# A hybrid attention block on one core: product 21 of a paired head moved between u and q, hooks moved by a product, and the first output block reordered

## The chip, the core and the metric

The kernel runs on one core of a Trainium2 chip: TensorE (matrix products into PSUM, an accumulator memory in banks of 512 fp32 values per partition), VectorE, ScalarE and GpSimd (element work), SyncE and GpSimd issue DMAs. The metric is the device time of one execution in microseconds; the kernel before ran three timed times, and once under the hardware profiler.

## The reference, cut to what matters

```python
h = _rmsnorm(x, norm_g[l])                      # x: (1, 512, 2048) float32
proj = h @ w_in[l]                              # q, k, v, z of both groups of heads, gates
...
qa = _rope(_heads(qa, 8, 128))                  # heads 0 to 7: three attentions, mixed by gates
o_a = gates[..., 0:1]*o_cmp + gates[..., 1:2]*o_sel + gates[..., 2:3]*o_win
y_a = o_a.reshape(B, S, WIDTH_A) * jax.nn.silu(za)
qb = _rope(_heads(qb, 16, 64))                  # two of these make one "head" of 128 columns
o_b = _banded_attention(qb, kb, vb, 128, sink)  # window of 128, a sink per head
y_b = o_b.reshape(B, S, WIDTH_B) * jax.nn.silu(zb)
x = x + jnp.concatenate([y_a, y_b], axis=-1) @ w_out[l]
return _rmsnorm(x, final_g)
```

All is fp32. The kernel splits each fp32 operand into a high and a low word and makes each product as three matrix products of words (`mm3`, L126 to L129: high x high, low x high, high x low).

## The kernel before, in words

The 512 tokens lie in SBUF as normalized words `xh`, `xl`. A first part (to 195 us) makes keys, values, compressed keys and gates. Then come 16 heads of 128 columns: 0 to 7 of the first kind, 8 to 15 of the second kind (two small heads side by side).

For heads 1 to 14 the q and the z projection are one 2 x 2 block product with seven multiplications in place of eight (a Strassen-Winograd scheme), in `pair(h)` at L685. The products are named p, 22, 21, 12, w, u, q. Each is 24 matmuls of 128 x 256 (`prod`, L661) on a sum of weight blocks. A weight block (128 x 1024) comes by DMA into a `raw` tile; `unit` splits it (ScalarE copies the high words `whi`, L641; VectorE subtracts for the low words `wlo`, L642); VectorE adds blocks to one another (`plus`, L698/L699). The seven products go into halves of two banks, `pa` and `pb`; ScalarE copies a product out (L731, L737, L747) or VectorE adds it to partial sums (L699). 22 is made first, then p, 21, 12, w, u, q. p, 12 and w lie in `pa`, 22, 21, u and q in `pb`. With u the query projection is whole: VectorE and GpSimd rotate it (L760 to L762), `q_split` makes words `qh`, `ql` (heads 1 to 7: ScalarE L501, GpSimd L502), `qb_split` the words `qs` of heads 8 on (ScalarE L870, VectorE L873, then four DMAs on SyncE's queue, L882, that move the low words to other partitions). `tags` hands out the five `raw` rooms; a room is free again when its last split or sum has read it. Heads up to 9 are narrow here (four rooms, sums made in place), heads 10 on wide (`h > 9`, five rooms, one more sum made by an accumulating DMA).

Behind its pair a head of the first kind runs `attn_a` (scores L565, softmax, transposes L603, value products L609 to L611). A head of the second kind is held: its parts are hung into the next head's pair as hooks, each issued behind a product (scores L903/L904 by `s0`, `s1`; divisions L922/L924; value products L942, L943, L948 by `k0` to `k3`, `end`). Head 15 has plain projections (`plain`, L775) with the same hooks.

Behind the last head comes the output projection. The first 512 columns (`wo0`, L1110) are plain: 8 units of 48 matmuls. Meanwhile `combos` (L1028) makes sums of y's blocks and their words, in place of y. Then `xs` rows are added to the products and squared (L1124 to L1127), and for n = 1 to 3 (L1149) the next 512 columns each are again seven products p, 22, 12, u, ... with weights from `wos`; `summed` (L1181) loads two blocks on top of one another (a load by SyncE, then an accumulating one by GpSimd, L1185), into tiles `ch`.

The written order is not the order of the engines: a scheduler with a simulated timeline orders each engine's instructions by what is ready in its model; `issue_after` binds an instruction behind another. PSUM is guarded bank by bank: a product that begins in a bank waits for what an engine still reads from that bank.

Of the kernel before, what the change touches and what calls it, by code (L numbers as in the profile page):

```python
# [17 lines left out]
P = 128  # L18
# [17 lines left out]
def hybrid_block(ctx, tc, xT, xtm, w0, w1s, w2s, wz, wq, wkb, wo0, wos, cw1, cw2, cpos, rope, tabs, sinks, gT, fg, out):  # L36
# [39 lines left out]
    raws = [0]  # L76
# [448 lines left out]
    pso = poa.enter_context(tc.tile_pool(name="pso", bufs=1, space=PSUM, side="left"))  # L525
    wks = ctx.enter_context(ExitStack())
# [146 lines left out]
    tags = ["raw2", "raw0", "raw1", "raw3"]  # L673
# [11 lines left out]
    def pair(h, early=(), hooks=None):  # L685
# [14 lines left out]

        if wide:
            c1, c2, c5, c3, c4 = tags
            tags[:] = c4, c1, c2, c3, c5
        else:
            c1, c2, c4, c3 = tags
            tags[:] = (c4, c1, c3, c2) if h < 9 else (c4, c1, "raw4", c3, c2)
        pa, pb = [psp.tile([P, S], F32, name="pj", tag="pj") for e in range(2)]
# [7 lines left out]
        if wide:  # L715
            d = wb.tile([P, 256], F32, name="dd", tag="dd")
        x1 = load(c1, 3)
        u0 = unit(x1)
        x2 = load(c2, 0)
        u3 = unit(x2)  # L720
        if wide:
            sm = load(c5, 0, 2)
        else:
# [17 lines left out]
        if wide:  # L741
            x4 = load(c4, 2, 3)
# [9 lines left out]
        plus(d, d, pa[:, H1])  # L752
# [3 lines left out]
        prod(pb[:, H1], u5, "u", True)  # L756
        plus(qv[:, H1], d, pb[:, H1])
# [56 lines left out]
    for h in range(8):  # L814
        if h < FIRST:
# [5 lines left out]
            with tc.issue_after(last["dma"]):  # L821
                first.append(load_quarter(wq[0], tags[0], 3))
                forms_back(0, lows)
                forms_back(1, lows)
            for c, quarter in zip(tags[1:], (0, 2, 1)):
# [28 lines left out]
    vb3 = wb.tile([P, P], F32, name="vb3")  # L854
    nc.sync.dma_start(cosB, ropeb[0])
# [11 lines left out]
    def qb_split(t1, direct=False):  # L867
# [3 lines left out]
        if not direct:  # L871
            lo = wk.tile([P, S], F32R, name="qlo", tag="t2", bufs=1)
            dve.tensor_tensor(out=lo, in0=t1, in1=q2[0].bitcast(F32), op=ALU.subtract)  # L873
        for v, qs in enumerate(q2):
            for half in range(2):
                r = half * 64 + v * 32
                d = half * 64 + 32 - v * 32
                if direct:
                    dve.tensor_tensor(out=qs[d:d + 32], in0=t1[r:r + 32], in1=qs[r:r + 32].bitcast(F32),
                                      op=ALU.subtract)  # L880
                else:
                    nc.sync.dma_start(qs[d:d + 32].bitcast(F32), lo[r:r + 32].bitcast(F32))  # L882
        return q2

    def attention(i, q2):
# [6 lines left out]
        def softmax(part):  # L892
# [26 lines left out]
            for e, v, ns in parts:  # L919
                tv = tts[2 * part + e][:, v, ns]  # L920
                if i < 6:
                    act.activation(tv, tv, AF.Copy, scale=dn[:, e, v:v + 1])  # L922
                else:
                    dve.tensor_scalar(tv, tv, dn[:, e, v:v + 1], None, op0=ALU.mult)  # L924
# [513 lines left out]
```

## Time and profile before

| | us |
|---|---|
| three timed executions | 831.44, 834.11, 838.43 (median 834.11) |
| the profiled execution | 830.96 |
| its span | 829.1 |
| TensorE clock granted, mean | 0.996 |
| matmuls busy (share of span) | 796.3 (96%) |
| weight loads busy | 746.1 (90%) |
| VectorE | 688.4 (83%) |
| ScalarE | 521.9 (63%) |
| GpSimd | 91.3 (11%) |

The profiled execution is one run, and its views are given in us from the start of its span. A matmul's row is longer than its share of TensorE's time, since matmuls are pipelined; what counts is the distance of two starts. Idle time of an engine is told with what ended it: `[0.84 <-PE pj L129]` is 0.84 us of idle time that ended when an instruction of line 129 on TensorE, writing `pj`, was done. PEld are the weight loads of TensorE. The stage of the paired heads is about 222 to 600 us, head 15 and the last held head 600 to 700, the output projection the rest.

### The profile page before, as it was taken

To read this page: it belongs to the slowest core of one execution; us is meant where nothing else is said; L and a number is where in the kernel's file an instruction comes from. 1 tells how busy PE (TensorE), PEld (TensorE's weight loads), DVE (VectorE), ACT (ScalarE), POOL (GpSimd) and SP (SyncE) were. 2 spreads that over 40 slices of the span, in tenths; PEclk is the share of its full clock that TensorE was granted. 3 is DMA by queue.
4 is the path that set the end of the run, shared out by engine and by line. 5 is a ranking of instruction groups with operands and counts; after the bars stand their busy time and mean duration, and the time that the engine had idled before them with its cause. 6 is when DMAs were issued, how large, how long until landed. Compare 5 with 4: busy or idle time off the path is not lost.

```text
span 829.1 us, 15441 instructions
## 1 busy us (share of the span) xinstructions
PE 796.3 (96%) x5782; PEld 746.1 (90%) x5782; DVE 688.4 (83%) x1283; ACT 521.9 (63%) x1088; POOL 91.3 (11%) x75
## 2 busy tenths in 40 slices
PE   8999999999999999999999999999999998899996
PEld 7788898988999999999999899899988887899996
DVE  6869785975798989997997898889987998678894
ACT  6734456662577867866777478676875657443545
POOL 3510002022010011010110012101110000100000
PEclk9999999999999999999999999999999999999999
DMA  8665886899712215323213585666674236697835
GB/s 308 210 204 166 277 283 209 250 307 359 251 44 95 77 42 165 109 61 113 85 58 115 159 205 153 168 174 153 179 261 158 77 102 245 189 262 192 267 66 203
DMA packets 60475, 145.03 MB, mean 175 GB/s; under 512 B 6257, under 2 KB 19825, under 8 KB 60401
## 3 DMA queue, kind: packets, MB, share of 16 engines
q1 hardware_dynamic: 56944, 132.00, 48.2%
q0 software_dynamic: 3168, 11.54, 8.2%
q8 instruction: 45, 0.74, 0.4%
q10 hardware_dynamic: 288, 0.52, 0.2%
q14 instruction: 30, 0.24, 0.1%
HBM read 121.65 MB, written 20.55 MB: 172 GB/s over the span
## 4 chain that ended last, share of the span: by engine, by line
PE 69%; DVE 10%; DMA 10%; ACT 4%; issue 4%; SPq 1%; POOL 1%; ACTq 0%; DVEq 0%; POOLq 0%
PE pj L127 12%; PE pj L129 12%; PE pj L128 12%; PE bank L129 4%; PE bank L128 3%; PE bank L127 3%; PE sp L565 3%; PE oa L128 3%; PE oa L129 3%; PE oa L127 3%; DMA rw<-wos 2%; DMA qs<-qlo 2%; DMA raw<-wq 1%; DVE wlo L642 1%; DMA ch<-wos 1%
## 5 line engine op out<-in xcount | busy, mean ns | idle before, releaser
L127 PE MATMUL pj<-xh,whi 128*128 128x256 f32 (+1 forms) x560 | 170.7, 305 | 2.7 <-ACT whi L641 1.5
L129 PE MATMUL pj<-xh,wlo 128*128 128x256 f32 (+1 forms) x560 | 170.1, 304 | 3.0 <-DVE wlo L642 2.9
L128 PE MATMUL pj<-xl,whi 128*128 128x256 f32 (+1 forms) x560 | 169.0, 302 | 0.0
L641 ACT ACTIVATE whi<-raw 128x1024 fp32r<-128x1024 f32 x98 | 102.8, 1054 | 46.7 <-PE pj L128 19.4
L642 DVE TENSOR_TENSOR wlo<-raw,whi 128x1024 fp32r<-128x1024 f32 x98 | 122.0, 1249 | 8.8 <-ACT whi L641 8.4
L129 PEld LDWEIGHTS pj<-xh,wlo 128*128 128x128 f32 x560 | 105.5, 188 | 8.9 <-DVE wlo L642 4.0
L127 PEld LDWEIGHTS pj<-xh,whi 128*128 128x128 f32 x560 | 105.5, 188 | 8.5 <-ACT whi L641 1.9
L128 PEld LDWEIGHTS pj<-xl,whi 128*128 128x128 f32 x560 | 105.4, 188 | 4.4 <-issue 0.2
L97 DVE TENSOR_TENSOR wlo<-raw,whi 128x512 fp32r<-128x512 f32 (+2 forms) x74 | 80.7, 1095 | 33.8 <-ACT whi L96 33.6
L96 ACT ACTIVATE whi<-raw 128x1024 fp32r<-128x1024 f32 (+1 forms) x73 | 65.3, 900 | 57.9 <-PE pj L128 14.9
L127 PE MATMUL pj<-pu,whi 128*128 128x256 f32 x224 | 63.9, 285 | 0.4 <-DVE zr L699 0.3
L129 PE MATMUL pj<-pu,wlo 128*128 128x256 f32 x224 | 63.4, 283 | 0.0
L128 PE MATMUL pj<-pu,whi 128*128 128x256 f32 x224 | 63.2, 282 | 0.0
L699 DVE TENSOR_TENSOR raw<-raw 128x1024 f32<-128x1024 f32 x46 | 58.0, 1261 | 0.2
L762 POOL TENSOR_TENSOR t<-t,t 128x512 f32<-128x512 f32 x14 | 24.4, 1745 | 248.1 <-DVE sums L584 79.6
L128 PE MATMUL oa<-wlo,xh 128*128 128x256 f32 (+1 forms) x168 | 50.3, 299 | 1.5 <-DVE wlo L1016 0.9
L127 PE MATMUL oa<-whi,xh 128*128 128x256 f32 (+1 forms) x168 | 50.0, 300 | 0.9 <-ACT whi L1015 0.9
L129 PE MATMUL oa<-whi,xl 128*128 128x256 f32 (+1 forms) x168 | 50.0, 299 | 0.0
L127 PEld LDWEIGHTS pj<-pu,whi 128*128 128x128 f32 x224 | 42.2, 189 | 1.4 <-DVE zr L699 1.3
L533 ACT ACTIVATE ph<-tp 128x512 fp32r<-128x512 f32 x56 | 32.1, 590 | 16.9 <-PE tp L936 8.6
L129 PEld LDWEIGHTS pj<-pu,wlo 128*128 128x128 f32 x224 | 42.3, 189 | 0.5 <-DVE wlo L642 0.2
L128 PEld LDWEIGHTS pj<-pu,whi 128*128 128x128 f32 x224 | 42.2, 188 | 0.1
(364 smaller groups left out, 2347.0 us busy)
## 6 DMA issues: line engine op xcount, KB each, us to landing
raw<-wq SPq DMA_DIRECT2D x65, 512.0 KB, 4.3
raw<-cw SPq DMA_DIRECT2D x16, 512.0 KB, 4.9
raw<-wos SPq DMA_DIRECT2D x12, 512.0 KB, 4.9
raw<-wq POOLq DMA_DIRECT2D x10, 512.0 KB, 5.6
rw<-wos SPq DMA_DIRECT2D x10, 512.0 KB, 5.7
xr<-xT SPq DMA_DIRECT2D x16, 256.0 KB, 5.3
raw<-w SPq DMA_DIRECT2D x8, 512.0 KB, 4.4
fd<-ft SPq DMA_DIRECT2D x4, 1024.0 KB, 5.8
```

Source lines behind the costliest of these rows:

```text
L96: last["hi"] = act.activation(hi[:, :width], rw[:, :width], AF.Copy).ins
L97: last["lo"] = dve.tensor_tensor(out=lo[:, :width], in0=rw[:, :width], in1=hi[:, :width].bitcast(F32), op=ALU.subtract).ins
L127: pe.matmul(ps, ah, bh, start=first, stop=False, skip_group_check=go_on)
L128: pe.matmul(ps, ah, bl, start=False, stop=False, skip_group_check=go_on)
L129: recent["mm"] = pe.matmul(ps, al, bh, start=False, stop=last, skip_group_check=go_on).ins
L533: act.activation(ph, tp, AF.Copy)
L565: pe.matmul(sp[:, a:b], qq[:, qs], kk[0][:, ko:ko + b - a], start=pi == 0, stop=pi == 2)
L641: act.activation(hi, src, AF.Copy)
L642: last["lo"] = dve.tensor_tensor(out=lo, in0=src, in1=hi.bitcast(F32), op=ALU.subtract).ins
L699: return dve.tensor_tensor(out=out, in0=a, in1=b, op=op).ins
L762: pool.tensor_tensor(out=qv, in0=qv, in1=t2, op=ALU.add)
```

## The change

In `pair`, the order of products becomes p, 22, 12, w, u, 21, q. u and q move to the half of the bank that p and 12 had, 21 stays with 22, and the two banks change roles from head to head. The hooks move with the order: what hung behind 21 now hangs behind 12, and so on, so that each hangs behind a product of the same number (third, fourth, ...). The order of loads and room tags follows. All divisions of the held heads are ScalarE's. Head 15's q words go through the four DMAs as those of heads 8 to 14 do. Behind the last head the tile `raw3` lies in a room that stays to the end; the first block sum of n = 1 is loaded into it (SyncE and accumulating GpSimd DMA) behind head 15's z; `combos` writes the words of u and q into rooms that are free since the last scores (`cmb`, `cmc`); and the additions of `xs` rows with their squares (`first_rows`) stand behind the splits of the second product's weights of n = 1.

```diff
@@ weights, pools
-        home = {"raw3": lambda: wk, "raw4": lambda: wb}.get(tag, lambda: wp)()
+        home = {"raw3": lambda: chp, "raw4": lambda: wb}.get(tag, lambda: wp)()
...
+    chp = ctx.enter_context(sb("chp"))
+    weights("raw3")
...
-    tags = ["raw2", "raw0", "raw1", "raw3"]
+    tags = ["raw0", "raw2", "raw1", "raw3"]
@@ pair
-        pa, pb = [psp.tile([P, S], F32, name="pj", tag="pj") for e in range(2)]
+        banks = [psp.tile([P, S], F32, name="pj", tag="pj") for e in range(2)]
+        pa, pb = banks if h % 2 else banks[::-1]
...
+        prod(pa[:, H0], u3, "p", True)
+        act.activation(d, pa[:, H0], AF.Copy)
         prod(pb[:, H0], u0, "22", True)
-        act.activation(d, pb[:, H0], AF.Copy, scale=-1.0)
-        x3 = load(c3, 1)
-        prod(pa[:, H0], u3, "p", True)
-        plus(d, d, pa[:, H0])
-        u2 = unit(x3)
-        prod(pb[:, H0], u2, "21", False)
-        act.activation(zr[:, H1], pb[:, H0], AF.Copy)
-        plus(jj, d, zr[:, H1])
-        after("21")
+        plus(d, d, pb[:, H0], ALU.subtract)
         u4 = unit(sm)
...
         plus(sm, sm, x1)
+        x3 = load(c3, 1)
         prod(pa[:, H0], u4, "12", False)
         act.activation(qv[:, H0], pa[:, H0], AF.Copy)
-        plus(jj, jj, qv[:, H0], ALU.subtract)
+        plus(jj, d, qv[:, H0], ALU.subtract)
         after("12")
         u1 = unit(x4)
         prod(pa[:, H1], u1, "w", True)
-        plus(d, d, pa[:, H1])
+        plus(qv[:, H1], d, pa[:, H1])
         after("w")
         u5 = unit(sm)
         plus(sm, sm, x3)
-        prod(pb[:, H1], u5, "u", True)
-        plus(qv[:, H1], d, pb[:, H1])
+        prod(pa[:, H0], u5, "u", True)
+        plus(qv[:, H1], qv[:, H1], pa[:, H0])
...
         qq = q_split(qv) if h < 8 else qb_split(qv)
+        after("u")
+        u2 = unit(x3)
+        prod(pb[:, H0], u2, "21", False)
+        act.activation(zr[:, H1], pb[:, H0], AF.Copy)
+        plus(jj, jj, zr[:, H1])
+        after("21")
         u6 = unit(sm)
-        after("u")
-        prod(pb[:, H1], u6, "q", False)
-        plus(jj, jj, pb[:, H1])
+        prod(pa[:, H0], u6, "q", False)
+        plus(jj, jj, pa[:, H0])
@@ heads 8 on
-                if i < 6:
-                    act.activation(tv, tv, AF.Copy, scale=dn[:, e, v:v + 1])
-                else:
-                    dve.tensor_scalar(tv, tv, dn[:, e, v:v + 1], None, op0=ALU.mult)
+                act.activation(tv, tv, AF.Copy, scale=dn[:, e, v:v + 1])
...
-            hooks = {"21": [j["s0"]], "12": [j["s1"]], "w": [j["k0"]], "u": [j["k2"], j["k3"]], "q": [j["k1"], end]}
+            hooks = {"12": [j["s0"]], "w": [j["s1"]], "u": [j["k0"]], "21": [j["k2"], j["k3"]], "q": [j["k1"], end]}
...
-    a15 = attention(7, qb_split(q_rope(qp, cosB, sinB, dve), True))
+    a15 = attention(7, qb_split(q_rope(qp, cosB, sinB, dve)))
@@ behind the last head
+    ch1 = weights("raw3")
+    with tc.issue_after(last["dma"]):
+        nc.sync.dma_start(ch1, wos[0][0, 0])
+    pool.dma_start(ch1, wos[0][2, 0], accum_op=ALU.add)
...
+    uq = {(nm, m): [(cmb if m < 4 else cmc).tile([P, 2, 256], F32R, name=f"{nm}{e}{m}") for e in "hl"]
+          for m in (2, 0, 6, 4) for nm in "qu"}
...
-        for nm, src in (("p", a11), ("u", a12), ("q", a21)):
+        for nm, src in (("p", a11), ("q", a21), ("u", a12)):
...
-    for t in range(NQ):
-        v = xs0[t // 2][:, t % 2, :]
-        dve.tensor_tensor(out=v, in0=acc[t], in1=v, op=ALU.add)
-        square(ssq[:, t, 1:2], v)
+    def first_rows():
+        for t in range(NQ):
+            v = xs0[t // 2][:, t % 2, :]
+            with tc.issue_after(last["lo"]):
+                dve.tensor_tensor(out=v, in0=acc[t], in1=v, op=ALU.add)
+            square(ssq[:, t, 1:2], v)
...
-            product(bb, [halves(r) for r in r22], "22", True)
+            u22 = [halves(r) for r in r22]
+            if n == 1:
+                first_rows()
+            product(bb, u22, "22", True)
         gg = scratch()
-        ch = summed(chain, 0, 2)
+        ch = summed(chain, 0, 2, [ch1] if n == 1 else ())
```

TensorE, last pair (head 14), kernel before, from the end of u to the start of q. `pj_7186` is `pb`; `pu11` are the words that u multiplies, `VH`, `VL` those of q; `tp` are transposes of the held head.

```order
L127 MATMUL pj_7186<-pu11_1364,whi_7424 128x256
L128 MATMUL pj_7186<-pu11_1364,whi_7424 128x256
L129 MATMUL pj_7186<-pu11_1364,wlo_7425 128x256
L936 MATMUL tp_7411<-ident_61,ttb_7288 128x128
L936 MATMUL tp_7411<-ident_61,ttb_7296 128x128
L936 MATMUL tp_7411<-ident_61,ttb_7288 128x128
L936 MATMUL tp_7411<-ident_61,ttb_7296 128x128
L127 MATMUL pj_7186<-VH_1383,whi_7469 128x256
L128 MATMUL pj_7186<-VL_1384,whi_7469 128x256
```

The change there. `pj_7193` is `pa`, which u has just left and q enters; `pj_7192` is `pb`.

```order
L129 MATMUL pj_7192<-xh_108,wlo_7447 128x256
L127 MATMUL pj_7192<-xh_108,whi_7446 128x256
L128 MATMUL pj_7192<-xl_109,whi_7446 128x256
L129 MATMUL pj_7192<-xh_108,wlo_7447 128x256
L127 MATMUL pj_7192<-xh_108,whi_7446 128x256
L128 MATMUL pj_7192<-xl_109,whi_7446 128x256
L129 MATMUL pj_7192<-xh_108,wlo_7447 128x256
L933 MATMUL tp_7433<-ident_61,ttb_7299 128x128
L933 MATMUL tp_7433<-ident_61,ttb_7307 128x128
L933 MATMUL tp_7433<-ident_61,ttb_7299 128x128
L933 MATMUL tp_7433<-ident_61,ttb_7307 128x128
L127 MATMUL pj_7193<-VH_1383,whi_7496 128x256
```

What moved: seven matmuls of 21 now stand between u and q, beside the four transposes; the other 17 of 21 stand ahead of u.

TensorE, a narrow pair of the change (head 4), from the end of 12 to the start of w. `pj_3545` is `pa` with 12 and then w, `pj_3544` is `pb` with 21; `sp` are scores of the head before.

```order
L129 MATMUL pj_3545<-xh_108,wlo_3614 128x256
L567 MATMUL sp_3442<-KH0_119,qh_3308 128x288
L567 MATMUL sp_3442<-KH0_119,qh_3308 128x512
L567 MATMUL sp_3442<-KL0_121,qh_3308 128x288
L567 MATMUL sp_3442<-KL0_121,qh_3308 128x512
L567 MATMUL sp_3442<-KH0_119,ql_3309 128x288
L567 MATMUL sp_3442<-KH0_119,ql_3309 128x512
L127 MATMUL pj_3544<-xh_108,whi_3715 128x256
L128 MATMUL pj_3544<-xl_109,whi_3715 128x256
L127 MATMUL pj_3545<-xh_108,whi_3647 128x256
```

What moved: before, 21 was whole ahead of 12; now its first two matmuls stand between 12's scores and w, the rest behind w.

VectorE, first output block behind the last head, kernel before. `xs00`, `xs01` are the rows to be added, `pl`, `ul`, `xl` low words of y, `wlo` those of weights (from `raw`: product p; from `rw`: 22; from `ch`: 12).

```order
L1126 TENSOR_TENSOR xs00_7951<-oa_7980,xs00_7951 128x512
L1126 TENSOR_TENSOR xs00_7951<-oa_7981,xs00_7951 128x512
L1016 TENSOR_TENSOR pl_7959<-y3_7549,ph_7958 128x512
L1126 TENSOR_TENSOR xs01_7952<-pj_7982,xs01_7952 128x512
L1126 TENSOR_TENSOR xs01_7952<-pj_7983,xs01_7952 128x512
L1016 TENSOR_TENSOR wlo_8316<-raw_8313,whi_8315 128x1024
L1016 TENSOR_TENSOR ul6_8273<-y3_7549,uh6_8272 128x512
L1016 TENSOR_TENSOR xl_109<-y3_7549,xh_108 128x2x256
L1016 TENSOR_TENSOR wlo_8376<-rw_8369,whi_8375 128x1024
L1016 TENSOR_TENSOR wlo_8380<-rw_8371,whi_8379 128x1024
L1016 TENSOR_TENSOR wlo_8440<-ch_8432,whi_8439 128x1024
```

The change there. `raw_7891` is the sum that is loaded early.

```order
L1018 TENSOR_TENSOR ul6_7983<-y3_7556,uh6_7982 128x512
L1018 TENSOR_TENSOR xl_109<-y3_7556,xh_108 128x2x256
L1018 TENSOR_TENSOR wlo_8379<-rw_8372,whi_8378 128x1024
L1018 TENSOR_TENSOR wlo_8383<-rw_8374,whi_8382 128x1024
L1130 TENSOR_TENSOR xs00_7966<-oa_8011,xs00_7966 128x512
L1130 TENSOR_TENSOR xs00_7966<-oa_8012,xs00_7966 128x512
L1130 TENSOR_TENSOR xs01_7967<-pj_8013,xs01_7967 128x512
L1130 TENSOR_TENSOR xs01_7967<-pj_8014,xs01_7967 128x512
L1018 TENSOR_TENSOR wlo_8452<-raw_7891,whi_8451 128x1024
```

What moved: the four additions stand behind the low words for 22 and ahead of those for 12; the low words for p and most of y's stand further up.

## Rows read from the trace of the kernel before

**Rows 1.** Page, part 1: busy us (share of span) and instructions of each engine.
```profile
PE 796.3 (96%) x5782; PEld 746.1 (90%) x5782; DVE 688.4 (83%) x1283; ACT 521.9 (63%) x1088; POOL 91.3 (11%) x75
```

**Rows 2.** Stretches: from:to and length, busy us (x instructions), TensorE clock, DMA share, GB/s.
```profile
222.00:600.00 378.00, 365.65 (x3029) 356.28 (x3029) 336.77 (x721) 277.25 (x663) 42.41 (x30) 1.00 0.42 121
300.00:330.00 30.00, 29.08 (x242) 28.45 (x242) 28.19 (x60) 21.62 (x55) 3.35 (x3) 1.00 0.35 116
625.00:675.00 50.00, 49.36 (x257) 41.47 (x256) 44.57 (x106) 31.84 (x69) 0.00 (x0) 1.00 0.33 104
700.00:725.00 25.00, 20.20 (x170) 19.41 (x169) 18.72 (x22) 13.21 (x20) 3.05 (x4) 1.00 0.74 230
725.00:750.00 25.00, 25.00 (x223) 25.00 (x222) 17.49 (x18) 12.75 (x19) 2.21 (x3) 1.00 1.01 274
```

**Rows 3.** Waits of TensorE: line <- releaser: us in total, times, longest.
```profile
PE oa L128 <- DVE wlo L1016: 3.9, 3, 2.0
PE pj L129 <- DVE wlo L642: 2.9, 4, 0.9
PE spb L903 <- DMA qs<-qlo: 2.5, 3, 1.2
PE pj L127 <- ACT whi L641: 1.5, 2, 0.9
PE oa L127 <- ACT whi L1015: 0.9, 1, 0.9
PE pj L127 <- DVE t L699: 0.8, 2, 0.6
```

**Rows 4.** Timeline, last pair, u to q: start, us, engine, line, operation, tiles [idle before <-releaser].
```profile
613.83 0.42 DVE L699 TENSOR_TENSOR t<-dd,pj 128x256 f32<-128x256 f32 x1 [0.84 <-PE pj L129]
614.30 0.38 PE L127 MATMUL pj<-VH,whi 128*128 128x256 f32 x1
```

**Rows 5.** Single lines: count, shortest/median/longest ns, first and last start, forms.
```profile
L641 ACT ACTIVATE whi<-raw x98: 1040/1054/1074, 199.3 to 607.7; 128x1024 fp32r<-128x1024 f32 x98
L731 ACT ACTIVATE t<-pj x9: 357/368/386, 214.6 to 461.1; 128x256 f32<-128x256 f32 x9
L565 PE MATMUL sp<-KH,qh x64: 274/295/398, 210.2 to 443.8; 128*128 128x288 f32 x32, 128*128 128x256 f32 x16, 128*128 128x512 f32 x16
L922 ACT ACTIVATE ttb<-ttb,sums x48: 384/495/508, 480.4 to 619.8; 128x256 f32<-128x256 f32 x36, 128x128 f32<-128x128 f32 x12
L879 DVE TENSOR_TENSOR qs<-t,qs x4: 679/684/686, 643.0 to 645.3; 32x512 fp32r<-32x512 f32 x4
```

**Rows 6.** Timeline, from product u (or its rotation) to scores: one narrow, one wide head.
```profile
385.52 0.28 PE L129 MATMUL pj<-pu,wlo 128*128 128x256 f32 x1
395.58 2.38 POOL L502 TENSOR_TENSOR ql<-t,qh 128x512 fp32r<-128x512 f32 x1 [2.06 <-ACT qh L501]
588.35 0.69 DVE L760 TENSOR_TENSOR t<-t,sinA 64x512 f32<-64x512 f32 x1
601.57 0.38 PE L903 MATMUL spb<-VH,qs 128*128 128x256 f32 x1 [1.10 <-DMA qs<-qlo]
```

**Rows 7.** Chain that ended last, the same wide head: start us, us, what.
```profile
596.62 4.91 DMA qs<-qlo
```

**Rows 8.** Timeline, first output block behind the last head: VectorE, GpSimd and TensorE.
```profile
702.92 1.27 DVE L1126 TENSOR_TENSOR xs<-pj,xs 128x512 f32<-128x512 f32 x2
703.85 1.79 POOL L1185 DMA_DIRECT2D ch<-wos  x2 [85.04 <-ACT whi L1015]
705.38 0.39 PE L128 MATMUL oa<-wlo,ph 128*128 128x256 f32 x1 [2.05 <-DVE wlo L1016]
716.00 1.23 DVE L1016 TENSOR_TENSOR wlo<-ch,whi 128x1024 fp32r<-128x1024 f32 x1 [3.92 <-ACT whi L1015]
717.28 0.39 PE L128 MATMUL oa<-wlo,xh 128*128 128x256 f32 x1 [0.85 <-DVE wlo L1016]
721.28 0.39 PE L128 MATMUL oa<-wlo,uh 128*128 128x256 f32 x1 [0.99 <-DVE wlo L1016]
```

More of the change, by code (lines that the diff above doesn't have):

```diff
@@ L716, in pair @@
             d = wb.tile([P, 256], F32, name="dd", tag="dd")
+        x2 = load(c2, 0)
+        u3 = unit(x2)
         x1 = load(c1, 3)
         u0 = unit(x1)
-        x2 = load(c2, 0)
-        u3 = unit(x2)
         if wide:
             sm = load(c5, 0, 2)
+            x4 = load(c4, 2, 3)
         else:
@@ L729, in pair @@
                 plus(x2, x2, x4)
+        prod(pa[:, H0], u3, "p", True)
+        act.activation(d, pa[:, H0], AF.Copy)
         prod(pb[:, H0], u0, "22", True)
-        act.activation(d, pb[:, H0], AF.Copy, scale=-1.0)
-        x3 = load(c3, 1)
-        prod(pa[:, H0], u3, "p", True)
-        plus(d, d, pa[:, H0])
-        u2 = unit(x3)
-        prod(pb[:, H0], u2, "21", False)
-        act.activation(zr[:, H1], pb[:, H0], AF.Copy)
-        plus(jj, d, zr[:, H1])
-        after("21")
+        plus(d, d, pb[:, H0], ALU.subtract)
         u4 = unit(sm)
-        if wide:
-            x4 = load(c4, 2, 3)
-        else:
+        if not wide:
             plus(x4, x4, x1)
         plus(sm, sm, x1)
+        x3 = load(c3, 1)
         prod(pa[:, H0], u4, "12", False)
         act.activation(qv[:, H0], pa[:, H0], AF.Copy)
-        plus(jj, jj, qv[:, H0], ALU.subtract)
+        plus(jj, d, qv[:, H0], ALU.subtract)
         after("12")
@@ L821, in hybrid_block @@
             with tc.issue_after(last["dma"]):
-                first.append(load_quarter(wq[0], tags[0], 3))
+                first.append(load_quarter(wq[0], tags[1], 0))
                 forms_back(0, lows)
                 forms_back(1, lows)
-            for c, quarter in zip(tags[1:], (0, 2, 1)):
+            for c, quarter in ((tags[0], 3), (tags[2], 2), (tags[3], 1)):
                 with tc.issue_after(last["dma"]):
@@ L854, in hybrid_block @@
     vb3 = wb.tile([P, P], F32, name="vb3")
+    wb.tile([P, 3, 2, 2], F32, name="sums", tag="sums", bufs=2)
+    wb.tile([P, 2, 256], F32, name="ttb", tag="ttb", bufs=4)
+    wb.tile([P, S], F32, name="ob", tag="ob")
     nc.sync.dma_start(cosB, ropeb[0])
@@ L870, in qb_split @@
             act.activation(qs, t1, AF.Copy)
-        if not direct:
-            lo = wk.tile([P, S], F32R, name="qlo", tag="t2", bufs=1)
-            dve.tensor_tensor(out=lo, in0=t1, in1=q2[0].bitcast(F32), op=ALU.subtract)
+        lo = wk.tile([P, S], F32R, name="qlo", tag="t2", bufs=1)
+        dve.tensor_tensor(out=lo, in0=t1, in1=q2[0].bitcast(F32), op=ALU.subtract)
         for v, qs in enumerate(q2):
@@ L877, in qb_split @@
                 d = half * 64 + 32 - v * 32
[L878 to L882, printed above, removed]
+                nc.sync.dma_start(qs[d:d + 32].bitcast(F32), lo[r:r + 32].bitcast(F32))
         return q2
@@ L1005, in hybrid_block @@
     cmb = ctx.enter_context(sb("cmb", side="right"))
+    cmc = ctx.enter_context(sb("cmc", side="right"))
     so = ctx.enter_context(sb("so"))
@@ L1033, in combos @@
         dve.tensor_tensor(out=a22, in0=a22, in1=a12, op=ALU.subtract)
-        for nm, src in (("p", a11), ("u", a12), ("q", a21)):
-            if nm == "p":
-                hi, lo = [w[:, m:m + 2] for w in pq]
-            else:
-                hi, lo = [cmb.tile([P, 2, 256], F32R, name=f"{nm}{e}{m}") for e in "hl"]
+        for nm, src in (("p", a11), ("q", a21), ("u", a12)):
+            hi, lo = [w[:, m:m + 2] for w in pq] if nm == "p" else uq[nm, m]
             split_to(hi, lo, src)
@@ L1178, in chain, with summed @@
         def chain():
-            return wr.tile([P, 1024], F32, name="ch", tag="ch", bufs=2)
-        def summed(tile_of, q1, q2):
-            got = []
-            for g in range(2):
+            raws[1] += 1
+            return weights("raw3") if raws[1] % 2 else wr.tile([P, 1024], F32, name="ch", tag="ch")
+        def summed(tile_of, q1, q2, got=()):
+            got = list(got)
+            for g in range(len(got), 2):
                 c = load(tile_of(), q1, g)
```

13 lines of the change are left out of this document (6 added, 7 removed).

## The prediction, made before the change was run

> **What bounds the kernel now.** First the page: TensorE's matmuls fill 796.3 of 829.1 us, VectorE 688.4, ScalarE 521.9 [rows 1]. The change adds no TensorE work (5761 matrix instructions before and after), so it can give back only TensorE's idle time, and 32.8 us is all there is. Then the busy time by stretches says where that idle time lies [rows 2]. The stage of the paired heads, 222 to 600 us, has 378 - 365.65 = 12.35 us of it, about 0.9 us for each of the 14 pairs. The first projection group behind the last head, 700 to 725, has 4.8 us in 25. From 725 to 750 there is none: 223 matmuls in 25.00 us, 112 ns each, the pitch I use below. In a typical pair VectorE is as full as TensorE: 28.19 us of 30 from 300 to 330. Last the waits of TensorE, which name what it stood still for [rows 3]: many small things, none over 4 us in all. In the pairs these are splits of weights (low words 2.9, high words 1.5), the q words that go through DMAs (2.5), the read of product u (0.8); behind the heads, low and high words of the output weights (3.9 and 0.9).
>
> **The pairs: q no longer waits for u's read.** Before, product q goes into the bank half that u has just left, with only transposes between, so that it starts when VectorE has read u. The last pair shows it: the read starts at 613.83 and takes 0.42, q's first matmul starts at 614.30, 0.05 us later [rows 4]. Over all pairs this wait is 0.8 us, in two of 14 [rows 3]. After, one to seven matmuls of product 21 and some transposes or value products stand there (the order of the last pair shows seven and four). Seven matmuls at 112 ns are 0.78, as long as the read with its start; one is not. Gain: 0.8, between 0 and 0.8.
>
> **The pairs: what 21 now waits for.** The order shows something the diff does not tell: the scheduler puts two matmuls of 21 directly behind 12 and its cover, then product w, then most of 21. Those two need the high words of 21's weights, which are written into the room that 12 has just freed, so ScalarE makes them only after 12. And the copy of 12, for which w waits (same bank), stands behind this split on ScalarE. A split of high words takes 1.05 us, the copy of a product 0.37 [rows 5]. Against that stands the cover on TensorE: nine score matmuls in three or four pairs, six in three, eight scores of a later head in one, more in the others. Scores come in three widths, 256, 288 and 512 columns [rows 5]; at the pitch of 112 ns for 256, and in proportion for the others, nine (three of each) are 1.4 us, six (three each of 288 and 512) 1.05, eight of 256 0.9; 21's two add 0.22. The need, from 12's end to w's start, is 1.05 + 0.37 + 0.05 = 1.47: nothing stays bare with nine, 0.2 with six, 0.35 with eight. That is 3 x 0.2 + 0.35, +1.0 us. The bounds are 0 (ScalarE, 277 us busy of 378 [rows 2], has got the split done meanwhile) and +5.9, the copy with its start bare in every pair, 14 x (0.37 + 0.05).
>
> The rule that speaks against this place: the Trainium skill, Perfetto Trace Analysis, section Optimizing Tensor Performance, Matmuls, wants independent groups of matmuls to rotate through the banks, so that emptying one overlaps the next. The change puts 12 and w next to each other in one bank, so by that rule each pair pays for the copy; it is the third rival below.
>
> **The pairs: q words and the rest.** The hooks keep their place by count, so the scores of the held head come after the third and fourth product as before. Between u's end and the first use of its q the new order has some 64 to 68 matmuls' worth of TensorE work in narrow heads (7.2 to 7.7 us), about 115 (12.6 to 13.6) in wide ones; before it was 7.1 to 11.5 and 12.3 to 16.5. The cover thus does not grow where it was short, and I take the 2.5 us of waits for these DMAs as staying. Bounds: -2.5 if all goes, and above, the second rival. Splits and additions come in another order (the sum of two weight blocks is needed as third product and no longer as fourth); work and counts are the same, and I cost it at 0 between -4 and +4, a third of the stage's idle time each way. The divisions of the last heads go from VectorE to ScalarE: 16 of them, 0.50 each [rows 5], are 8 us on an engine that is idle for 18 of the 50 us from 625 to 675 [rows 2]. Cost 0; without this cover, the 8 us less what TensorE finds to do meanwhile. The last head's q words come by four DMAs instead of four VectorE instructions. Those took 4 x 0.68 = 2.7 [rows 5], a DMA of the wide pairs 4.91 from issue to landing [rows 7]: 0, since the products of z still to be made lie between, or the 2.2 of difference if they do not cover it.
>
> **Behind the last head.** Before, the four additions of rows (0.64 each by their pitch) and splits of y stand on VectorE ahead of low words that TensorE needs: the last two, at 702.92, stand right before the split whose end lets the matmul at 705.38 go, after 2.05 us [rows 8]. The change puts the additions behind the second group's splits and splits y earlier, into room that is free since the last scores. By then y's words are made while the products of the first output block run, so both the 0.90 wait for high words and the 2.05 fall away: -2.95. Next in line is product 12 of this block: its second half waited 0.85 at 717.28, for low words that were made at 716.00, after VectorE had been idle for 3.92 us; what was late were the two accumulating loads that GpSimd issued from 703.85 on [rows 8]. The first half is now loaded while head 15 runs, so one of the two is gone from this queue: -0.5, between 0 and -0.85. The wait of 0.99 at 721.28 [rows 8] is for a sum and splits that follow on VectorE, and stays. The additions, 2.6 us of VectorE, now meet its gap ahead of 716.00, 3.92 us wide [rows 8]: no cost; if they hit the splits of 12 instead, that wait comes back with up to 2.6.
>
> **Sum.** On the profiled execution: 830.96 - 0.8 + 1.0 - 2.95 - 0.5 = 827.7. Four executions of the kernel before are known, 830.96, 831.44, 834.11 and 838.43; their middle is 832.8, and the median of the three timed ones 834.1, 3.1 above the profiled one. I put the -3.25 on 832.8: **829.5 us**.
>
> **The rivals.**
> First, faster: the idle time that the order can give back is larger than the waits say. The rows of weight loads show 378 - 356.28 = 21.7 us without a load in the pair stage, against 12.35 without a matmul [rows 2]. If the new order, which gives 21 as a filler behind 12 and u, takes away half of the 12.35 (6.2) with the 3.45 behind the heads, the time is 832.8 - 9.6 = 823. For it: the filler's weights are ready early. Against: VectorE is 94% busy there. The Trainium skill, Perfetto Trace Analysis, section Identifying the Most-Contended Engine, calls matmul busy time a poor measure and wants that of LDWEIGHTS; by it there would be more to gain than I take.
> Second, slower: scores wait for q. In one narrow head u's last matmul starts at 385.52 and the low words of q end at 395.58 + 2.38 = 397.96, 12.2 us later; in a wide one it was 13.2 us from 588.35 to the landing at 601.53, and the scores at 601.57 had stood still for 1.10 [rows 6, 7]. Over all heads I find 7.2 to 12.7 and 10.3 to 16.6. Where the order leaves 7.5, a chain that stays at its mean of 10.2 is waited for 2.7 us in six narrow heads, 16 us in all: 849. It decides against the kernel once the mean wait of 12 pairs exceeds 0.9 us. Against it: the chain was long because VectorE served other work first, and the order of the change has it served sooner.
> Third, the bank: the copy of 12 is bare in all 14 pairs, 5.9 in place of 1.0: 834.4.
> Fourth, the change does little of what it says: 21 stands mostly ahead of u, VectorE stays the bound of a pair, and waits move from one split to the next. The tail's gain is half lost to the moved additions: 831.5 to 834.
>
> **How the numbers follow.** Chances: forecast 0.40 (its own range 825 to 833), first rival 0.20, second 0.13, third 0.07, fourth 0.20. A measurement of this kernel can tell about 1% from no change, 8.3 us, since its own runs spread by 7. Below 824.5 lies most of the first rival and a little of the forecast: 0.20. Above 841 lies the second and a little of the others: 0.14. The rest, 0.66, is within 1%. The range takes in the forecast, the third and fourth, the first down to 821 and the second's mildest part: 821 to 841, leaving out 0.1 above and 0.06 below.
>
> **What would show it.** In the changed kernel's waits: q has no row for u's read; w has a row for the copy of 12 (or 21 for its high words) of 1 to 2 us; the DMAs of the q words keep 2 to 3 us; the output block's low words shrink from 3.9 to about 1.5. The stretch of the first output block shows 2 to 4 us less idle time, the stage of the pairs 11 to 14. Wrong would I be if the pairs' idle time falls below 8 or rises over 18, or if GpSimd's low words of q, in narrow heads, stand ahead of TensorE's scores as the last thing awaited.

## The result: 1.06% slower, and the profile after

The changed kernel takes 841.16 us (median of 14 executions, 839.05 to 846.72), the kernel before 833.78 (14, 830.56 to 838.87): ratio 1.0106, 95% interval 1.0085 to 1.0127. Forecast was 829.5, no change that can be told. The profiled execution took 841.44, its span is 839.7, 10.6 above the one of before.

The page, part 1, of the changed kernel (as [rows 1]):

```profile
PE 802.2 (96%) x5782; PEld 753.1 (90%) x5782; DVE 693.3 (83%) x1264; ACT 528.4 (63%) x1104; POOL 90.7 (11%) x75
```

The work is the same, 5782 matmuls in the records of both (the prediction has 5761, a number that no profile shows). The waits of TensorE (as [rows 3]; line <- releaser: us in total, times, longest), the first seven:

```profile
PE sp L567 <- DVE sums L573: 8.9, 6, 1.9
PE sp L567 <- DVE sums L586: 4.2, 3, 1.4
PE pj L127 <- ACT zr L764: 3.0, 3, 1.1
PE spb L903 <- DMA qs<-qlo: 2.6, 1, 2.6
PE oa L128 <- DVE wlo L1018: 2.2, 3, 0.9
PE oa L127 <- ACT whi L1017: 1.9, 2, 1.7
PE bank L127 <- ACT whi L96: 1.3, 3, 0.5
```

`sp` are the scores of heads 0 to 7. Before, they waited once:

```profile
PE sp L565 <- DVE sums L571: 0.4, 1, 0.4
```

Now they wait nine times, 13.1 us, until VectorE had read the scores of the group before out of the same banks. The read of u has no row any more. The third row is the copy of product 21, for which the next pair's first product waits.

One of these waits in full. VectorE's timeline (start, us, line, operation, tiles, [idle before]):

```profile
310.62 1.22 DVE L644 TENSOR_TENSOR wlo<-raw,whi 128x1024 fp32r<-128x1024 f32 x1
311.87 0.42 DVE L701 TENSOR_TENSOR t<-t,pj 128x256 f32<-128x256 f32 x1
312.21 1.22 DVE L644 TENSOR_TENSOR wlo<-raw,whi 128x1024 fp32r<-128x1024 f32 x1
313.34 0.69 DVE L514 SCALAR_TENSOR_TENSOR st<-op,st 128x512 f32<-128x512 f32 x1
313.94 0.18 DVE L569 CUSTOM_DVE_ANT_0 tc__3376<-sp,tab 128x32 f32<-128x32 f32 x1
...
314.39 0.42 DVE L573 CUSTOM_DVE_ANT_0 tt<-sp,tab 128x256 f32<-128x256 f32 x1
```

and TensorE's, the same place:

```profile
311.51 0.36 PE L567 MATMUL sp<-KH,ql 128*128 128x256 f32 x1
...
312.77 0.28 PE L129 MATMUL pj<-xh,wlo 128*128 128x256 f32 x1
314.97 0.60 PE L567 MATMUL sp<-KH,qh 128*128 128x288 f32 x2 [1.92 <-DVE sums L573]
```

The second score group ends at 311.9. Only ten matmuls of product 12 follow, then the third group, which goes into the same banks. VectorE is not idle in between: a sum, a split and the end of the head before stand ahead of the read in its queue, and the read begins at 313.94. In the order before, 4.8 us of other work lay between these two groups; now it is 1.2 us. Six of the nine waits are of this kind, one in each of heads 2 to 7, with ten or three matmuls between two groups; they make 10.0 of the 13.1 us. The other three, 1.64, 0.91 and 0.59 us in heads 0 and 1, have 72, 15 and 23 matmuls between the groups, so there the distance alone does not explain the wait.

Behind the last head, SyncE's queue, ScalarE, and TensorE of the changed kernel:

```profile
705.04 0.89 SPq L1124 DMA_DIRECT2D xs<-xtm  x2
706.02 2.66 SPq L1164 DMA_DIRECT2D rw<-wos  x2
...
713.46 1.06 ACT L1017 ACTIVATE whi<-rw 128x1024 fp32r<-128x1024 f32 x1 [2.09 <-DMA rw<-wos]
...
714.57 0.38 PE L127 MATMUL oa<-whi,xh 128*128 128x256 f32 x1 [1.66 <-ACT whi L1017]
```

Of the two waits that the prediction names at this place, the one of 2.05, for low words of product p, is gone. The one of 0.90 was already product 22's, for the high words of its weights (`whi` from `rw`; kernel before, ScalarE and TensorE):

```profile
701.85 1.99 ACT L1015 ACTIVATE whi<-rw 128x1024 fp32r<-128x1024 f32 x2
702.95 0.38 PE L127 MATMUL oa<-whi,xh 128*128 128x256 f32 x1 [0.90 <-ACT whi L1015]
```

It is now 1.66, with 0.87 for low words behind it, since the weights land at 713.4. Their loads stand behind those of the rows `xs`, and both behind head 15's y, which is later: y is added up 40.4 us after the first output matmul, 34.9 before. This is the row of its sum in the kernel before, in the change, and what ScalarE did ahead of it in the change:

```profile
691.35 0.69 DVE L514 SCALAR_TENSOR_TENSOR y<-ob,st 128x512 f32<-128x512 f32 x1
```

```profile
701.19 1.06 ACT L1017 ACTIVATE whi<-raw 128x1024 fp32r<-128x1024 f32 x1 [2.94 <-issue]
702.27 0.59 ACT L952 ACTIVATE ob<-opb 64x512 f32<-64x512 f32 x1
...
704.26 0.69 DVE L514 SCALAR_TENSOR_TENSOR y<-ob,st 128x512 f32<-128x512 f32 x1
```

Busy time by stretches (from:to and length, then busy us of PE, PEld, DVE, ACT, POOL, TensorE clock, DMA share, GB/s; as [rows 2]):

```profile
222.00:600.00 378.00, 361.95 (x2992) 353.04 (x2992) 337.85 (x706) 273.85 (x652) 42.06 (x30) 1.00 0.41 118
443.00:447.00 4.00, 4.00 (x18) 3.77 (x19) 3.86 (x12) 1.99 (x8) 0.00 (x0) 0.57 0.49 151
716.00:720.00 4.00, 4.00 (x22) 4.00 (x23) 4.00 (x6) 3.58 (x9) 0.52 (x1) 0.57 0.98 383
```

TensorE is idle for 16.05 us of the 378, 3.7 more than before, and gets less done in them. The second and third rows are what standstills cost on top: after the wait that ended at 442.89 (1.93 us) the granted clock is half for 3.4 us, and again after the waits of 1.66 and 0.87 us behind the last head. Between 200 us and the last matmul there are three such stretches in this profile and none in that of before; in the second profiles (r12 and r11, below) there are four with the change and three before.

For the experiments I read three marks from each profile: the last matmul of the eighth pair's q, the first matmul of the output projection, the last matmul of all. Differences of starts (the last one: to its end):

| profile | order in heads 1 to 9 | to the mark of pair 8 | from there to the first output matmul | from there to the last matmul |
|---|---|---|---|---|
| before; again (r11) | old | 455.4; 455.6 | 201.0; 203.8 | 164.8; 164.6 |
| change; again (r12) | new | 460.8; 461.7 | 203.0; 202.4 | 168.5; 166.8 |
| r1 | old | 454.9 | 203.9 | 166.6 |
| r2 | new | 462.6 | 205.8 | 163.9 |
| r3 | old | 455.8 | 210.2 | 169.6 |
| r4 | new, scores apart | 455.6 | 209.9 | 166.7 |
| r5 | new | 462.5 | 202.7 | 165.9 |
| r6 | new, scores apart | 455.9 | 204.1 | 166.1 |
| r7 | old | 454.4 | 202.9 | 163.8 |
| r8 | old | 456.5 | 205.8 | 167.9 |
| r9 | old | 455.1 | 204.7 | 162.4 |
| r10 | new, scores apart | 455.9 | 203.5 | 164.2 |

### The profile page after: what moved, and what is told of

It reads as the page before. It is cut to its first block, busy times and chain, and to the rows that moved or that the text cites. A ratio compares the mean times of both kernels' runs of the same rounds, so it can differ in the third digit from the quotient of the medians.

```text
span 839.7 us, 15409 instructions
## 1 busy us (share of the span) xinstructions
PE 802.2 (96%) x5782; PEld 753.1 (90%) x5782; DVE 693.3 (83%) x1264; ACT 528.4 (63%) x1104; POOL 90.7 (11%) x75
## 4 chain that ended last, share of the span: by engine, by line
PE 53%; DVE 22%; DMA 11%; ACT 6%; issue 6%; SPq 1%; POOL 0%; DVEq 0%; ACTq 0%
PE pj L127 9%; PE pj L128 9%; PE pj L129 9%; DVE wlo L644 5%; PE oa L128 4%; PE oa L129 4%; PE oa L127 4%; DVE raw L701 2%; PE sp L567 2%; PE bank L129 2%; PE bank L127 2%; PE bank L128 2%; DVE wlo L97 2%; DVE zr L701 2%; DVE tt L573 1%
## 5 line engine op out<-in xcount | busy, mean ns | idle before, releaser
L644 DVE TENSOR_TENSOR wlo<-raw,whi 128x1024 fp32r<-128x1024 f32 x98 | 128.7, 1323 | 10.5 <-ACT whi L643 10.1
L97 DVE TENSOR_TENSOR wlo<-raw,whi 128x512 fp32r<-128x512 f32 (+2 forms) x74 | 83.2, 1130 | 29.5 <-ACT whi L96 29.2
L536 DVE TENSOR_TENSOR pl<-tp,ph 128x512 fp32r<-128x512 f32 x56 | 37.8, 685 | 5.8 <-ACT ph L535 5.7
```

Of the source, the lines that this page charges most:

```text
L97: last["lo"] = dve.tensor_tensor(out=lo[:, :width], in0=rw[:, :width], in1=hi[:, :width].bitcast(F32), op=ALU.subtract).ins
L536: dve.tensor_tensor(out=pl, in0=tp, in1=ph.bitcast(F32), op=ALU.subtract)
L644: last["lo"] = dve.tensor_tensor(out=lo, in0=src, in1=hi.bitcast(F32), op=ALU.subtract).ins
```

## The experiments

Ratios are to the kernel before, run on the same chip (833.8 us beside the change, 832.0 to 832.3 in the experiments).

**r1_old_pairs.** The change without its pairs: `pair`, the first loads, the tags and the hooks are those of before.

```diff
-            hooks = {"12": [j["s0"]], "w": [j["s1"]], "u": [j["k0"]], "21": [j["k2"], j["k3"]], "q": [j["k1"], end]}
+            hooks = {"21": [j["s0"]], "12": [j["s1"]], "w": [j["k0"]], "u": [j["k2"], j["k3"]], "q": [j["k1"], end]}
...
-        prod(pa[:, H0], u3, "p", True)
+        prod(pb[:, H0], u0, "22", True)
```

> The change with the paired heads put back (old order of products, old banks, old hooks and rooms); all edits behind the last head stay. Theory 1 (score groups stand too close behind one another in the narrow pairs, so that TensorE waits until VectorE has read the score banks): about the time before or a little less, ratio 0.996 to 1.001 to the kernel before, no waits of scores for VectorE's sums over 1 us. Theory 2 (the loss is behind the last head): still 1.005 to 1.009. Theory 3 (VectorE simply has no room, waits turn up wherever the order is touched): 0.998 to 1.003, as with theory 1; the next kernels tell these apart.

Measured: 835.86, ratio 1.0030 (1.0004 to 1.0056). The scores wait for VectorE's sums once, 0.3 us. Most of the loss is in the pairs; but what is left stands above theory 1's bound (its interval begins below that), so some seems to be behind the last head too.

**r2_new_pairs.** The opposite: the kernel before with the new pairs alone (the same lines the other way round).

> The kernel before with the new pairs alone (order, banks, hooks, rooms); nothing else of the change. Theory 1: 1.007 to 1.012, with some 10 to 13 us of waits of scores for VectorE's sums. Theory 2: 0.998 to 1.003. Theory 3: as theory 1.

Measured: 843.86, ratio 1.0137 (1.0090 to 1.0184). Scores wait 13.3 us in all, nine times. The ratio is above theory 1's range, whose upper end its wide interval takes in. The pairs alone cost as much as the whole change.

**r3_narrow_old.** Which pairs: old order in heads 1 to 9, new in 10 to 14.

```diff
+    def pair(h, early=(), hooks=None):
+        return (pair_old if h <= 9 else pair_new)(h, early, hooks)
```

> The change, but heads 1 to 9 with the old order of products; the wide heads 10 to 14 and everything behind them as changed. Theory 1: the loss goes with the narrow pairs, ratio 0.999 to 1.004, scores wait under 1 us. Theory 2: 1.005 to 1.009. Rival within the pairs (the wide heads' q words, one wait of 2.6 us and a clock fall): 1.004 to 1.010, and r1_old_pairs lower than this by at least 0.004.

Measured: 844.20, ratio 1.0122 (1.0076 to 1.0168): against theory 1 by its time. The profile tells why it can't decide. Its narrow stage ends at 455.8, as before, with 0.3 us of waits of scores; but pair 10, where the orders meet, takes 33 us in place of 25 to 28. ScalarE's row there:

```profile
491.01 1.06 ACT L643 ACTIVATE whi<-raw 128x1024 fp32r<-128x1024 f32 x1 [6.47 <-DMA raw<-wq]
```

Weights came late at the seam; TensorE stood still for 4.36 us behind it and ran at half clock after. The kernel says something on the narrow stage, nothing on the whole.

**r4_scores_apart.** The change, with the scores of heads 0 to 6 tied to products of the next pair (the expectation says 1 to 6; the code takes head 0 too). The attention of a head becomes a generator that stops before its second, third and fourth score group:

```diff
+                if qt:
+                    yield
                 for pi, (qq, kk) in enumerate(((qh, KH), (qh, KL), (ql, KH))):
...
-        attn_a(h, *qq, st)
+        part = attn_a(h, *qq, st)
+        for _ in range(4 if h == 7 else 1):
+            next(part, None)
+        scores = {nm: [lambda part=part: next(part, None)] for nm in ("p", "12", "w")}
```

> The change, but the score groups of heads 1 to 6 hung behind products of the next pair (the second group not before p, the third not before 12, the fourth not before w), so that they cannot stand close together. Theory 1: the waits of scores for VectorE's sums fall from 13 to under 6 us, and the time by 3 to 7 us, ratio 1.001 to 1.006. Theory 3 (VectorE is the bound of the narrow pair): those waits fall, but others (low words, copies) take their place, ratio 1.008 to 1.012.

Measured: 843.66, ratio 1.0117 (1.0070 to 1.0164). By its time it lies in theory 3's range and against theory 1, but again pair 10 lost 7 us (TensorE waits there for divisions and for splits of weights that came late, and runs 6.8 us at half clock). In the stage in question the waits of scores are 4.2 us, and the eighth pair's q ends at 455.6 in place of 460.8. Other waits did come there, as theory 3 has it: 4.7 us from 200 us to this mark, 3.3 of them for high words, against 0.3 in the change and 4.9 before. But they did not take the time back, which speaks against theory 3.

**r5_wide_old** and **r6_apart_wide_old** make the clean pair: old order in the wide heads, changed tail, new order in the narrow ones; r6 has the scores apart, r5 not.

```diff
+        return (pair_old if h > 9 else pair_new)(h, early, hooks)
```

> The change, but the wide heads 10 to 14 with the old order of products; heads 1 to 9 and all behind the last head as changed. Theory 1 (in the narrow pairs the score groups follow one another too closely): the loss stays, ratio 1.006 to 1.011, the stretch from the first narrow pair's q to the eighth's some 225 to 227 us (221 before, 226 with the change), 11 to 14 us of waits of scores. Rival (the wide pairs' waits for a copy and for q words): 1.001 to 1.006.

> As r5_wide_old, with the score groups of heads 1 to 6 hung behind p, 12 and w of the next pair. In r4_scores_apart this brought the narrow stretch from 226 to 220.5 us, but pair 10 lost 7 us to late weights. Theory 1: the narrow stretch 219 to 223 us, waits of scores under 6 us, ratio 1.000 to 1.005, that is 3 to 7 us below r5_wide_old, unless pair 10 is late again (then its stretch is over 30 us and shows it). If VectorE is the bound, the narrow stretch stays at 225 to 227.

Measured: r5 841.72, ratio 1.0113 (1.0090 to 1.0136), 13.7 us of waits of scores, eighth q at 462.5; r6 835.16, ratio 1.0046 (1.0022 to 1.0070), eighth q at 455.9. The scores' rows of the waits, r5 and then r6:

```profile
PE sp L567 <- DVE sums L573: 9.5, 6, 2.2
PE sp L567 <- DVE sums L586: 4.2, 3, 1.4
```

```profile
PE sp L569 <- DVE sums L575: 4.4, 4, 2.2
```

Pair 10 takes 27.4 us in r5 and 30.2 in r6, the latter a little over the 30 us that the expectation names; in r6 TensorE waits there 2.3 us for a sum of VectorE's. Taking the score groups apart gives back 0.67% (5.6 us), 6.6 us in the profiles up to the eighth q; the one thing moved with it are the loads of keys and values for heads 4 to 7, a pair later. What is left of the waits is heads 0 and 1 (3.7 us), whose groups lie as in r5, and 0.7 in head 3: the six waits of heads 2 to 7 went from 10.0 us to that. From 200 us to the eighth q TensorE is idle for 14.1 us in r5 and 9.2 in r6 (before 5.4). The wide heads' order, old here, makes no difference: r5 stands where the change stands.

**r7_tail_div_vector.** r1 with the divisions of the last heads on VectorE, as before.

```diff
-                act.activation(tv, tv, AF.Copy, scale=dn[:, e, v:v + 1])
+                if i < 6:
+                    act.activation(tv, tv, AF.Copy, scale=dn[:, e, v:v + 1])
+                else:
+                    dve.tensor_scalar(tv, tv, dn[:, e, v:v + 1], None, op0=ALU.mult)
```

> As r1_old_pairs (old pairs, all edits behind the last head), with the divisions of the last heads back on VectorE. Theory 4 (the divisions on ScalarE make the last head's y late, and with it the weights of the output block, whose room it frees): y of head 15 is added up 34 to 37 us after the first output matmul (35 before, 40 with the change), the wait for the high words of product 22 is under 0.8 us (1.7 with the change), ratio 0.996 to 1.001. Rival (the new places of splits and loads make it late themselves): y 39 to 41 us after, ratio 1.001 to 1.005.

Measured: 831.95, ratio 0.9995 (0.9968 to 1.0022). Head 15's y is added up 36.3 us after the first output matmul (r1: 40.4). Product 22 waits no more, as theory 4 has it (r1: 1.70 for high words, 0.88 for low ones). A row of 1.6 us for high words remains, but it is product 12's, whose second half comes late into `ch`:

```profile
714.54 1.06 ACT L1020 ACTIVATE whi<-ch 128x1024 fp32r<-128x1024 f32 x1 [4.49 <-DMA ch<-wos]
715.65 0.38 PE L127 MATMUL oa<-whi,xh 128*128 128x256 f32 x1 [1.58 <-ACT whi L1020]
```

The divisions cost 0.35% (r1 less r7, 2.9 us; the two intervals just overlap). The way from the first output matmul to the last shrank from 166.6 to 163.8, TensorE's idle time in it from 5.9 to 3.9 us; r7 also has one stretch at half clock less there (1.7 us).

**r8_div_scalar_only.** The kernel before with that one edit in the other direction.

> The kernel before with all divisions of the heads 8 to 15 on ScalarE and nothing else of the change. Theory 4: y of head 15 is added up 38 to 41 us after the first output matmul (35 before), ratio 1.000 to 1.005. Rival (the divisions are hidden): 34 to 36 us, ratio 0.998 to 1.002.

Measured: 834.09, ratio 1.0014 (0.9991 to 1.0037), y 37.1 us after. Inconclusive by its time, and y lies between the two ranges, nearer to theory 4's. TensorE is idle for 7.2 us from the first output matmul to the last, where the same tail without this edit has 5.5 and 4.4 (before, twice) and 4.1 (r2): that speaks for theory 4. Why so little of it shows in the time, these runs don't show.

**r9_rows_behind_weights.** r7 with the loads of `xs` moved behind those of 22's weights.

```diff
         r22 = [load(rw(), 3, g) for g in range(2)]
+        if n == 1:
+            for T in range(2):
+                with tc.issue_after(last["dma"]):
+                    nc.sync.dma_start(xs0[T], xtm[:, 2 * T:2 * T + 2, 0:512])
         load_rows()
```

> As r7_tail_div_vector (old pairs, edits behind the last head, divisions on VectorE), with the two loads of the rows xs moved behind the two loads of product 22's weights on SyncE's queue, since the additions that need the rows now come later. Theory 5 (what is left of the tail's wait is 22's weights, which queue behind the rows): the wait for 22's high words falls from 1.6 us to under 0.6, ratio 0.995 to 0.999, faster than both kernels. Rival (the room of these weights comes free too late, whatever the queue): still 1.2 to 1.8 us, ratio 0.998 to 1.002.

Measured: 831.79, ratio 0.9987 (0.9962 to 1.0013). The wait that this was to take away was not there: in r7 product 22 waited for nothing, and the row of 1.6 us was product 12's. That one is 1.2 us here. So theory 5 is not tested by it. r9 is the fastest of all these kernels by its median and 1.2% below the change, but can't be told from the kernel before.

**r10_all_mended.** New order with scores apart in heads 1 to 9, old in the wide ones, divisions on VectorE, rows behind the weights.

> As r6_apart_wide_old (new order in heads 1 to 9 with the score groups hung apart, old order in heads 10 to 14), with the divisions back on VectorE and the loads of the rows behind those of 22's weights. Theories 1, 4 and 5 together: r6 (1.0046) less some 0.003 for the divisions less 0.001 to 0.002 for the loads: 0.998 to 1.003. If the two causes were not separate, it stays at 1.003 to 1.006.

Measured: 833.66, ratio 1.0017 (0.9988 to 1.0045). Taken away together, the two causes take the loss away, and the ratio lies where separate causes would put it; but its interval reaches into the other range, and r10 also has the old order in the wide heads (which made no difference in r5) and r9's loads. From r6 to r10 it is 0.29%, close to the 0.35% from r1 to r7.

**r11_before_again, r12_change_again.** Second profiles of both kernels.

> The kernel before, unchanged, profiled a second time. If the spacing of matmuls in the output blocks (113 ns in one profile, 118 in the other) belongs to the execution and not to the kernel, it may be either here, and changes only at a standstill of TensorE; the narrow stretch (first to eighth pair's q) is 220 to 224 us, as before, with under 1 us of waits of scores.

> The changed kernel, unchanged, profiled a second time. The narrow stretch again 225 to 227 us with 12 to 14 us of waits of scores; behind the last head again a wait of 1 to 2 us for the high words of product 22; the spacing of matmuls in the output blocks may be 113 or 118 ns.

Measured: 833.83 and 840.05. The scores wait 13.0 us in the change again, and the eighth q ends at 461.7 (455.6 before). Product 22 waits 1.46 us for high words in the change again. The narrow stretch came out a little above the range for both (224.7 and 227.7). The spacing of matmuls in the output blocks is told below.

## Why the prediction was wrong, step by step

**The step that failed** is the one on what 21 now waits for: "Against that stands the cover on TensorE: nine score matmuls in three or four pairs, six in three". I priced the wait of 21's first matmuls and of w behind these scores (+1.0 us), and took the scores themselves as work that runs when its turn comes. They were the wait. The two effects that I priced are indeed small (0.9 us for high words, no row for the copy of 12), but the order had moved the score groups next to one another: in heads 2 to 7 a group of six or nine score matmuls stands ten or three matmuls behind the group before, in the same banks, and VectorE, which I had noted as full in just this stage, reads that group behind a split or a sum of weight blocks and the end of a head. I looked at what was queued behind the scores and not at what they themselves wait for. Measured: 13.1 us of waits, while other waits of the stage went (TensorE's idle time from 200 us to the eighth q is 13.5 us, 5.4 before), and 5 to 7 us of time, where the sum had +1.0. The order shows it (the distance of two score groups), and VectorE's share of 94% was in [rows 2].

**Divisions on ScalarE, "cost 0".** Wrong by 2.9 us (r1 against r7). The 18 idle us of ScalarE in [rows 2] are an average of the stretch; the divisions of head 15 stand on the one chain that matters there. With VectorE the last of them starts some 4 us after the first output matmul, on ScalarE 10.5; transposes, products and y follow, and behind y stand the loads of the next weights. These are the last four on VectorE before, and in the change what they need (VectorE) and what stands ahead of them in ScalarE's queue:

```profile
659.78 1.14 DVE L924 TENSOR_SCALAR ttb<-ttb,sums 128x256 f32<-128x256 f32 x4
```

```profile
667.73 0.18 DVE L918 RECIPROCAL sums<-sums 128x4 f32<-128x4 f32 x1
667.40 4.85 ACT L987 ACTIVATE xh<-y 128x1024 fp32r<-128x1024 f32 x5
672.15 1.04 ACT L96 ACTIVATE whi<-raw 128x1024 fp32r<-128x1024 f32 x1
673.10 1.70 ACT L921 ACTIVATE ttb<-ttb,sums 128x256 f32<-128x256 f32 x4
```

The divisors are there at 667.9; five copies of y and a split of weights keep the divisions until 673.1.

**Behind the last head, -3.45.** Of this only the 2.05 came. The 0.90 was misread: I took it to go with y's words, but it was product 22's wait for its weights, and it grew to 1.66 and 0.87, since these weights queue behind the rows and behind y. "Next in line" was thus 22, and product 12's second half did not get faster either: 0.88 in place of 0.85, and 1.92 with 0.86 in the second profile. In all TensorE is idle from the first output matmul to the last for 4.6 and 6.2 us (change, and again) and for 5.5 and 4.4 before, where the sum had 3.45 less. The stretch became 2 to 4 us longer. Of the 3.7 between the first profiles none is waits; 1.7 is the clock and the rest the spacing of matmuls that is told at the end. Of the 2.2 between the second ones, which have the same spacing there, 1.7 are waits. Without the divisions (r7, r9, r10) TensorE is idle for 3.9, 2.5 and 3.7 us, and the stretch is 0.4 to 2.4 us shorter than before: no more than the spacing alone can make, so a gain of the tail is not shown.

**q no longer waits for u's read, -0.8.** Right: there is no row for it in either profile of the change.

**q words, 2.5 us staying.** Right in size (2.6 and 2.1), but in one wait in place of three, and that one is followed by 3.4 us at half clock.

**Copy of 21.** Not in the sum: the next pair's first product goes into the bank that 21 leaves, and waited for its copy three times, 3.0 us. The rest of the pairs' waits went down by more than that (from the eighth q to the output projection TensorE is idle for 8.7 us before, 7.7 in the change), so that the wide heads came out even.

**The rivals.** The first and the fourth lie at 834 us and below, the measurement above them. The second (slower, by scores that wait for q) has the right sign, the right instructions and the wrong mechanism: the scores waited for their banks, not for their words. The third, the copy of 12 bare, did not come. The sentence from the Trainium skill (Perfetto Trace Analysis, section Optimizing Tensor Performance, Matmuls), that independent groups should rotate through the banks, so that emptying one overlaps the next, did bear on this kernel: not where I put it, at 12 and w, but at the scores, which have one set of banks. The trace agrees with it there: 10.0 us of waits in heads 2 to 7, where groups follow closely, 0.7 in the same heads with the groups apart.

**The clock** was in no term. Over all executions its mean is 0.9891 in the change (14), and before it is 0.9927, 0.9919 and 0.9928 (17, 28 and 23 executions beside the experiments). At half clock TensorE loses half of the time, so 0.0028 to 0.0037 of 840 us is 2.4 to 3.1 us: an estimate from these means, a third to two fifths of the 7.4 us of loss. It is a part of the losses above and not one beside them.

**Range and chances.** 841.2 lies 0.2 us above the range; slower had 0.14, and the mechanism was none of the rivals. The terms that I set at zero had bounds for their own cost, not for what becomes late when the order closes up. My signs of being wrong did not show either: idle time of the pairs over 18 us was one, and it is 16.05, since time lost inside a stretch with fixed ends pushes work out of it (2992 matmuls in it, 3029 before).

What stays open: why the weights of pair 10 come late in r3 and r4 (r4 has no seam between two orders, so the seam alone is not it; the transfers of heads 8 on lie in the same stretch); how much of the 2.9 us for the divisions comes by way of y; why heads 0 and 1 wait with their score groups far apart; and whether r9 is faster than the kernel before.

## What to carry to other kernels

Work that is counted as cover (it is to keep TensorE busy during a wait) must be asked the same questions as the work it covers: which bank or room does it write, who reads that last, and how far in that reader's queue does the read stand. In a new order measure the distance between two users of the same bank before anything else. And idle time of an engine in a stretch pays for a moved operation only if the operation is not on the chain that frees the next room.

## What the runs showed of the hardware

A standstill of TensorE can cost more than its length. In the first profile of the change the clock fell to half (the 1.2 GHz level) for 3.4 us after waits of 1.93, 2.58 and 1.66 with 0.87; after two others of 1.92 and 1.93 (at 315 and 379 us) it did not, while in the second profile it fell at those two places and not after one of 1.92 at 445 us. Half of 3.4 us, 1.7 us of work, is lost by each.

Matmuls of one form (128 x 256) have two spacings, 113 and 118 ns, at full clock, that last for hundreds of matmuls in the output blocks. What makes one change into the other the runs do not show: not only a standstill, as I had expected for r11, since in the first profile of the kernel before it goes from 118 to 113 at 235.5 us with no gap. In the same 65 us of the output blocks the change's first profile, its second, and the second of the kernel before show (busy us and count of matmuls come first):

```profile
735.00:800.00 65.00, 65.00 (x554) 65.00 (x553) 52.02 (x60) 30.64 (x43) 5.63 (x7) 1.00 0.84 234
```

```profile
735.00:800.00 65.00, 65.00 (x576) 65.00 (x575) 53.32 (x62) 32.77 (x44) 6.08 (x7) 1.00 0.84 235
```

```profile
735.00:800.00 65.00, 65.00 (x576) 65.00 (x575) 53.56 (x61) 32.91 (x45) 6.09 (x7) 1.00 0.77 222
```

All are without a gap, and 22 matmuls apart, 2.5 us. In these 65 us two of the 14 profiles have 554 matmuls (the change's first and r3), one has 567 (r7), the others 575 or 576. So the spacing belongs to the execution and not to the kernel. The 2.5 us are more than the 1.7 us between the tails of the change's two profiles, of which the second has more waits. Two profiles alone, one of each kernel, would have put it down to the change.
